# Recurrent block: both square roots together, the gate branch in five banks, its output gated in pairs of blocks

## The chip, the cores and the metric

The kernel runs on one core of one Trainium2 chip. The metric is device time in microseconds (us) of one execution; of several runs the median is taken.

## What is computed

Two layers of a decoder trunk on one sequence of 256 tokens with 1024 channels, all in float32. The first layer is attention and a dense feed-forward block; the second is a recurrent block and a feed-forward block of eight experts of which each token takes two. The change lies in the recurrent block alone. With D_RNN = 1280, in ten blocks of 128 channels, the reference has there:

```
proj = h @ w_in
gate_branch, u = proj[..., :D_RNN], proj[..., D_RNN:]
conv = conv_b + sum_j u_pad[:, j:j + s] * conv_w[j]            # width 4, causal
r = sigmoid(einsum(conv blocks, w_a) + b_a)
i = sigmoid(einsum(conv blocks, w_x) + b_x)
log_a = -RG_C * r * softplus(-lam)
a = exp(log_a)
mult = sqrt(-expm1(2 * log_a))
hs = linear recurrence over s of (a, mult * i * conv)
y = gelu(gate_branch) * hs
return y @ w_out
```

## The kernel before

Each matrix product is made of three float32r products: the operands are split into a rounded part (`whi`, `hThi`, `y` and so on, made by `ACTIVATE` on ScalarE at L386 or by `CAST` on VectorE at L388) and a remainder (`wlo`, made by a subtraction on VectorE at L389), and `mm3` (L403 to L405) adds up high times high, low times high and high times low. All weights come through one stream, `ws`: SyncE loads pages of two pieces of 128x1024 into six buffers, `step` splits the pieces ahead of their use into pairs of tiles, and `ws.done` gives a used pair back and splits the next. The program's text is the order: each engine runs its instructions in the order in which the code issues them and waits for semaphores of the others.

The loop at L841 has 20 rounds. Rounds 0 to 9 make the branch `u` (weights "lu"), its convolution and the gates r and i, two rounds late. Rounds 10 to 19, called m = 0 to 9 here, make the gate branch (weights "lg"): each product is 128x256, two of them share one PSUM bank, and `gbk[m]` keeps the bank until `gelu(m)` (L827) has read both halves into `ge`. The banks come from `wbank()`, a ring of four named "B" that the convolution and gate products use too.

Beside these matmuls the table `beside` puts, round by round, what the other engines do: `exp_tanh` (ScalarE) makes a and, in `rg`, what stands under the root; `recur(g)` for the two groups of five blocks takes the root on ScalarE (L808), multiplies twice on VectorE (L809, L810) and scans along the sequence (L812); `gelu` takes a bank; and `gated(a, z)` multiplies the scan's blocks a to z-1 by `ge` (L819, VectorE), rounds the product into the tile `y` (L386, ScalarE) and makes the remainder (L389, VectorE). Behind `beside`, `ws.done` splits the next weights, on ScalarE too unless m is 2, 4 or 6. ScalarE loads a table when the function changes to one of another set: roots and GeLU are in different sets, rounding is in every set.

After the loop comes `gated(8, 10)`, and then the output projection: ten weights "lo", called n = 0 to 9 here, of 12 matmuls each, three into each of four banks. Its banks (`y_banks`) are, in the order in which each weight writes them, `y0`, `y1` and two named `t`. `gate_rows` (L336) stands behind n = 4. The last two weights are kept for `finish`, which also keeps TensorE busy with a few repeated matmuls (`warm`, L424) while the norm is taken. Then the expert layer follows.

The pieces that set the order:

```
    ws.act = m not in (2, 4, 6)
    ws.done(ada=4)
...
    def y_banks():
        return [[bank("y0"), bank("y1")], [bank("t", 2), bank("t", 2)]]
```

Of the kernel before, what the change touches and what calls it, by code (L numbers as in the profile page):

```python
# [13 lines left out]
AF = mybir.ActivationFunctionType  # L14
# [116 lines left out]
def trunk_kernel(ctx, tc, xin, cbc, sm_d, at_d, wd, wm, out, stage=9):  # L131
    nc = tc.nc
    ctx.enter_context(tc.manual_schedule())
    V, A, T, G, SY = nc.vector, nc.scalar, nc.tensor, nc.gpsimd, nc.sync
# [7 lines left out]
    def bank(tag, bufs=1, dt=F32, shape=(P, 512)):  # L142
        return ps.tile(list(shape), dt, name=tag, tag=tag, bufs=bufs)

    def wbank():
        return bank("B", 4)
# [177 lines left out]
    def gate_cols(layer, which, gi):  # L324
        g = gcol["g"] = tmp.tile([P, 8], F32, name="gcol", bufs=1)
        m, bias = mods(layer, which)
        V.tensor_tensor(g, m, bias, op=ALU.add)
        V.tensor_tensor(g, g, norm_g(layer, gi), op=ALU.mult)
# [16 lines left out]
    def rstd(parts):  # L345
        v = tmp.tile([P, 1], F32, name="var", bufs=4)
        V.scalar_tensor_tensor(v, parts[:, 0:1], EPS, parts[:, 1:2], op0=ALU.add, op1=ALU.add)
        r = tmp.tile([P, 1], F32, name="rstd", bufs=4)
        G.tensor_tensor(r, v, mhalf[:, 0:1], op=ALU.pow)
        return r  # L350

    def sumsq(src_halves):
        parts = tmp.tile([P, 2], F32, name="parts", bufs=4)
        for h in range(2):
            sq = tmp.tile([P, 512], BF16, name="sq", bufs=1)
            A.activation(sq, src_halves[h], AF.Square, scale=1.0 / 32, accum_out=parts[:, h:h + 1])
        return parts
# [26 lines left out]
    def split(hi, lo, v32, act=False):  # L384
        if act:
            A.activation(hi, v32, AF.Copy)  # L386
        else:
            V.tensor_copy(hi, v32)  # L388
        V.tensor_tensor(lo, v32, hi.bitcast(F32), op=ALU.subtract)  # L389
# [17 lines left out]
    def wstat(o, w, hi, lo):  # L407
        wh, wl = w[:2]
        for k in range(KT):
            c = slice(k * P, (k + 1) * P)  # L410
            mm3(o, wh[:, c], wl[:, c], hi[:, k], lo[:, k], k == 0, k == KT - 1)
# [112 lines left out]
    s4 = const.tile([P, N_RNN], F32, name="s4")  # L524
# [45 lines left out]
    for i in range(16):  # L570
        w = ws.next()
        kind, j = w[2]
        b = wbank()
# [180 lines left out]
    def spare(tag, w=2 * SUB, pool=None, bufs=1):  # L754
# [6 lines left out]
    rg, aa = [[poolR.tile([P, 5, S], F32, name=f"{t}{g}", tag=f"{t}{g}") for g in range(2)]  # L761
              for t in ("rg", "aa")]
# [6 lines left out]
    def conv_step(n, b):  # L769
        u = b[:, :S]  # L770
        cv = conv[:, n]
        A.activation(cv, u, AF.Identity, scale=cw[:, 30 + n:31 + n], bias=cb_[:, n:n + 1])
        for j in (2, 1, 0):
            sft = 3 - j
            V.scalar_tensor_tensor(cv[:, sft:], u[:, :S - sft], cw[:, j * 10 + n:j * 10 + n + 1], cv[:, sft:],
                                   op0=ALU.mult, op1=ALU.add)
# [3 lines left out]
    def conv_split(n):  # L780
        ch = poolR.tile([P, S], F32R, name="ch", bufs=2)
        cl = poolR.tile([P, S], F32R, name="cl", bufs=2)
        split(ch, cl, conv[:, n], True)
        chl[n] = ch, cl

    def gates_mm(n):
        w = axw[n // 4]
        b = wbank()
        ch, cl = chl.pop(n)
        for g in range(2):  # L790
            c = slice((n % 4) * 256 + g * P, (n % 4) * 256 + g * P + P)
            mm3(b[:, g * S:(g + 1) * S], w[0][:, c], w[1][:, c], ch, cl, True, True)
        return b

    def gates_act(n, b):
        A.activation(rg[n // 5][:, n % 5], b[:, :S], AF.Sigmoid, bias=C("rb_a")[:, n:n + 1])
        ig = poolR.tile([P, S], F32, name="ig", bufs=2)
        A.activation(ig, b[:, S:], AF.Sigmoid, bias=C("rb_x")[:, n:n + 1])
        V.tensor_tensor(conv[:, n], conv[:, n], ig, op=ALU.mult)
        if n in (3, 7, 9):  # L800
            ws.done()

    ys = {}

    def recur(g):

        r, a_, c = rg[g], aa[g], conv[:, 5 * g:5 * g + 5]
        A.activation(r, r, AF.Sqrt)  # L808
        V.scalar_tensor_tensor(r, a_, 1.0, r, op0=ALU.add, op1=ALU.mult)  # L809
        V.tensor_tensor(r, r, c, op=ALU.mult)  # L810
        V.memset(a_[:, :, 0:1], 0.0)
        V.tensor_tensor_scan(*[t.rearrange("p n s -> p (n s)") for t in (c, a_, r)], 0.0,  # L812
                             op0=ALU.mult, op1=ALU.add)

    def gated(a, z):
        g = a // 5
        if a % 5 == 0:
            ys[g] = [poolR.tile([P, 5, S], F32R, name="y", tag=f"{t}{g}") for t in ("rg", "aa")]
        V.tensor_tensor(conv[:, a:z], conv[:, a:z], ge[:, a:z], op=ALU.mult)  # L819
        split(*[t[:, a - 5 * g:z - 5 * g] for t in ys[g]], conv[:, a:z], True)  # L820

    def exp_tanh(f, dst, scale, g):
        for i in range(5):
            n = 5 * g + i
            A.activation(dst[g][:, i], rg[g][:, i], f, scale=scale[:, n:n + 1])

    def gelu(n):  # L827
        A.activation(ge[:, n:n + 2], gbk.pop(n).rearrange("p (a b) -> p a b", a=2), AF.Gelu_apprx_tanh)  # L828
# [1 line left out]
    beside = {  # L830
        2: [lambda: exp_tanh(AF.Exp, aa, s8, 0)],
        3: [lambda: exp_tanh(AF.Exp, aa, s8, 1), lambda: gate_cols(1, 2, 1)],
        4: [lambda: exp_tanh(AF.Tanh, rg, s4, 0)],
        5: [lambda: exp_tanh(AF.Tanh, rg, s4, 1), lambda: recur(0)],
        6: [lambda: gelu(0), lambda: gelu(2), lambda: gated(0, 4)],
        7: [lambda: recur(1), lambda: gelu(4), lambda: gated(4, 5)],
        8: [lambda: gelu(6), lambda: gated(5, 8)],
        9: [lambda: gelu(8)],
    }
    gbk = {}  # L840
    for n in range(2 * N_RNN):  # L841
        ws.cap = 5 if n < N_RNN else DENSE_AHEAD
        if n in (2, 6, N_RNN):
            axw.append(ws.next("ax"))
        if n < N_RNN:
            w = ws.next("lu")
            b = wbank()
            wstat(b[:, :S], w, hi, lo)
        else:
            m = n - N_RNN  # L850
            w = ws.next("lg")
            if m % 2 == 0:
                b = gbk[m] = wbank()
            wstat(b[:, (m % 2) * S:(m % 2 + 1) * S], w, hi, lo)
        if 2 <= n < N_RNN + 2:
            gb = gates_mm(n - 2)
        if 1 <= n <= N_RNN:
            conv_split(n - 1)
        if n < N_RNN:
            conv_step(n, b)  # L860
        if 2 <= n < N_RNN + 2:
            gates_act(n - 2, gb)
        if n < N_RNN:
            ws.done()
        else:
            for f in beside.get(m, []):
                f()
            ws.act = m not in (2, 4, 6)
            ws.done(ada=4)
# [615 lines left out]
    with tc.If(flag > 0):  # L1485
# [14 lines left out]
        for tt in range(2):  # L1500
            r = rstd(sumsq([x[:, tt, :512], x[:, tt, 512:]]))
# [5 lines left out]
        with tc.For_i(0, N_EXP) as e:  # L1507
# [17 lines left out]
            m = Moe(Stream(pg, kd), False)  # L1525
# [154 lines left out]
```

## Time and profile before

| | |
|---|---|
| median of three runs | 1446.88 us |
| the three runs | 1446.87, 1446.88 and 1448.28 us |
| the profiled execution, its own time | 1448.85 us |
| its span in the trace | 1447.0 us |
| busy in the span: TensorE / VectorE / ScalarE | 1386.4 / 900.6 / 708.3 us |
| mean granted TensorE clock | 0.989 |
| the stretch of the change | from 431.7 us (table load for a) to 488.8 us (last projection matmul) |

The times in the trace run from the start of the span. A row of a timeline tells when an instruction began and, in brackets, how long its engine had been idle and which instruction ended that. Instructions of one engine overlap a little: the distance of two starts is the price of one in a row of many, the duration is what another engine has to wait.

### The profile page before, as it was taken

The page shows a single profiled execution, that of the slowest core. Times are in us where ns is not written, and L with a number is a line of the kernel's source. Part 1 is how long each engine was busy: PE and PEld are TensorE (multiplying, and loading weights), DVE is VectorE, ACT ScalarE, POOL GpSimd, SP SyncE. Part 2 cuts the span into 40 slices and gives each one's busy share as a digit, 9 for nine tenths or more (in the row PEclk, how much of TensorE's full clock was granted, in tenths as well). Part 3 has the DMA queues.
Part 4 walks back from the last instruction along what each step waited for, and adds up shares of the span by engine and source line. Part 5 has one row for each costly group of instructions (what it writes and reads, how often), then busy time and mean ns, then how long its engine had stood idle before and what let it go on. Part 6 is the DMA issues. An engine that isn't in the chain of part 4 may idle for free.

```text
span 1447.0 us, 21766 instructions
## 1 busy us (share of the span) xinstructions
PE 1386.4 (96%) x8325; PEld 1025.5 (71%) x8325; DVE 900.6 (62%) x1277; ACT 708.3 (49%) x1030; POOL 45.9 (3%) x62
## 2 busy tenths in 40 slices
PE   4998999999898899999999999999999999999997
PEld 3895589999797678887777767766566566665652
DVE  6887588875698889888666766754333343333321
ACT  3535455444586677976565656743232232321312
POOL 0105300000000000000000000000000000000000
PEclk9999999999999999999999999999999999999999
DMA  9876578886254988699999999999999999998991
GB/s 392 318 271 238 221 274 324 337 313 259 89 181 169 357 323 306 225 359 365 372 397 402 410 386 420 384 382 406 409 391 402 391 365 404 391 404 334 381 371 57
DMA packets 76991, 476.86 MB, mean 330 GB/s; under 512 B 8528, under 2 KB 8528, under 8 KB 28880
## 3 DMA queue, kind: packets, MB, share of 16 engines
q1 hardware_dynamic: 76880, 475.40, 84.1%
q8 instruction: 67, 1.10, 0.3%
q14 instruction: 44, 0.36, 0.1%
HBM read 474.32 MB, written 1.05 MB: 329 GB/s over the span
## 4 chain that ended last, share of the span: by engine, by line
PE 54%; DMA 2%; DVE 1%; issue 1%; ACT 0%; ACTq 0%
PE B L1061 18%; PE y L1061 7%; PE B L403 7%; PE B L405 6%; PE B L404 6%; PE y L405 2%; PE y L403 2%; PE y L404 2%; PE t L1150 2%; DMA raw<-in_wm_dram 2%; PE t L1334 1%; DVE wlo L389 1%; PE t L1039 0%; PE t L1040 0%; PE B L1444 0%
## 5 line engine op out<-in xcount | busy, mean ns | idle before, releaser
L389 DVE TENSOR_TENSOR wlo<-raw,whi 128x1024 fp32r<-128x1024 f32 x459 | 551.2, 1222 | 278.8 <-ACT whi L386 234.4
L386 ACT ACTIVATE whi<-raw 128x1024 fp32r<-128x1024 f32 x456 | 473.3, 1057 | 263.9 <-PE B L405 181.5
L1061 PE MATMUL B<-raw,xTc 128*64 128x256 f32 x1792 | 205.3, 382 | 0.0
L403 PE MATMUL B<-hThi,whi 128*128 128x256 f32 x640 | 181.8, 284 | 2.7 <-ACT ge L828 1.7
L404 PE MATMUL B<-hTlo,whi 128*128 128x256 f32 x640 | 181.2, 283 | 0.6
L403 PE MATMUL B<-whi,xTh 128*128 128x512 f32 x448 | 181.1, 404 | 0.0
L405 PE MATMUL B<-hThi,wlo 128*128 128x256 f32 x640 | 179.2, 280 | 0.0
L404 PE MATMUL B<-wlo,xTh 128*128 128x512 f32 x448 | 177.1, 395 | 0.3 <-DVE wlo L389 0.2
L1061 PEld LDWEIGHTS B<-raw,xTc 128*64 128x64 f32 x1792 | 124.3, 137 | 74.5 <-issue 16.8
L405 PE MATMUL B<-whi,xTl 128*128 128x512 f32 x448 | 176.6, 394 | 0.0
L403 PEld LDWEIGHTS B<-hThi,whi 128*128 128x128 f32 x640 | 120.9, 189 | 4.1 <-ACT ge L828 1.9
L404 PEld LDWEIGHTS B<-hTlo,whi 128*128 128x128 f32 x640 | 120.6, 188 | 3.6 <-DVE hTlo L389 2.7
L405 PEld LDWEIGHTS B<-hThi,wlo 128*128 128x128 f32 x640 | 120.5, 188 | 0.0
L212 DVE CUSTOM_DVE_ANT_0 raw<-raw,cond 128x1024 f32<-128x1024 f32 x96 | 114.4, 1223 | 0.0
L403 PEld LDWEIGHTS B<-whi,xTh 128*128 128x128 f32 x448 | 84.1, 188 | 30.6 <-issue 12.8
L1061 PE MATMUL y<-raw,hTc 128*64 128x512 f32 x448 | 101.9, 596 | 0.0
L405 PEld LDWEIGHTS B<-whi,xTl 128*128 128x128 f32 x448 | 84.1, 188 | 19.4
L404 PEld LDWEIGHTS B<-wlo,xTh 128*128 128x128 f32 x448 | 84.2, 188 | 19.2 <-DVE wlo L389 2.0
L1138 ACT ACTIVATE sg<-B 128x512 f32<-128x512 f32 x35 | 20.8, 595 | 99.1 <-PE B L1061 99.1
L1061 PEld LDWEIGHTS y<-raw,hTc 128*64 128x64 f32 x448 | 30.6, 137 | 54.4 <-issue 52.3
L403 PE MATMUL y<-whi,hTh 128*128 128x512 f32 x168 | 67.4, 401 | 0.0
L405 PE MATMUL y<-whi,hTl 128*128 128x512 f32 x168 | 66.5, 396 | 0.2 <-DVE hTl L1161 0.2
(322 smaller groups left out, 1646.9 us busy)
## 6 DMA issues: line engine op xcount, KB each, us to landing
raw<-in_wm_dram SPq DMA_DIRECT2D x261, 1024.0 KB, 8.8
raw<-in_wd_dram SPq DMA_DIRECT2D x114, 1024.0 KB, 6.5
raw<-in_wm_dram SPq DMA_DIRECT2D x150, 512.0 KB, 8.3
x<-in_x_dram SPq DMA_DIRECT2D x1, 1024.0 KB, 5.2
out_dram<-res SPq DMA_DIRECT2D x4, 256.0 KB, 2.8
sm<-in_sm_dram SPq DMA_DIRECT2D x1, 548.5 KB, 6.8
cond<-in_c_dram SPq DMA_DIRECT2D x1, 512.0 KB, 6.0
at<-in_at_dram SPq DMA_DIRECT2D x1, 320.0 KB, 7.0
```

The source lines that it names most:

```text
L212: V.tensor_tensor_reduce(src, src, cond, 1.0, 0.0, op0=ALU.mult, op1=ALU.add, accum_out=modc[:, col:col + 1])
L386: A.activation(hi, v32, AF.Copy)
L389: V.tensor_tensor(lo, v32, hi.bitcast(F32), op=ALU.subtract)
L403: T.matmul(o, lh, rh, start=start, stop=False)
L404: T.matmul(o, lh, rl, start=False, stop=False)
L405: T.matmul(o, ll, rh, start=False, stop=stop)
L1061: T.matmul(o[64 * t:64 * t + 64], xs, w[:, t * n:t * n + n], start=start, stop=stop)
L1138: A.activation(g[t], ub[t], AF.Copy)
L1150: T.transpose(b[:, j * P:(j + 1) * P], a[t][:, j * P:(j + 1) * P], ident)
L1334: T.matmul(b, u.pt[t][r, tt * P:(tt + 1) * P], yr[r, j], start=j == 0, stop=j == 1)
```

## The change

The root becomes a function of its own, and both roots stand together in m = 5, the two calls that make what stands under them in m = 4. GeLU and gating are spread: one bank of GeLU and then the blocks that it completes, in six pieces of one or two blocks instead of four pieces of one to four. The second recurrence stands behind the first two pairs. The banks of m = 6 and m = 8 are `y0` and `y1` instead of two of the ring.

```
--- before.py
+++ after.py
@@ -802,10 +802,12 @@
 
     ys = {}
 
+    def root(g):
+        A.activation(rg[g], rg[g], AF.Sqrt)
+
     def recur(g):
 
         r, a_, c = rg[g], aa[g], conv[:, 5 * g:5 * g + 5]
-        A.activation(r, r, AF.Sqrt)
         V.scalar_tensor_tensor(r, a_, 1.0, r, op0=ALU.add, op1=ALU.mult)
         V.tensor_tensor(r, r, c, op=ALU.mult)
         V.memset(a_[:, :, 0:1], 0.0)
@@ -830,12 +832,12 @@
     beside = {
         2: [lambda: exp_tanh(AF.Exp, aa, s8, 0)],
         3: [lambda: exp_tanh(AF.Exp, aa, s8, 1), lambda: gate_cols(1, 2, 1)],
-        4: [lambda: exp_tanh(AF.Tanh, rg, s4, 0)],
-        5: [lambda: exp_tanh(AF.Tanh, rg, s4, 1), lambda: recur(0)],
-        6: [lambda: gelu(0), lambda: gelu(2), lambda: gated(0, 4)],
-        7: [lambda: recur(1), lambda: gelu(4), lambda: gated(4, 5)],
-        8: [lambda: gelu(6), lambda: gated(5, 8)],
-        9: [lambda: gelu(8)],
+        4: [lambda: exp_tanh(AF.Tanh, rg, s4, 0), lambda: exp_tanh(AF.Tanh, rg, s4, 1)],
+        5: [lambda: root(0), lambda: root(1), lambda: recur(0)],
+        6: [lambda: gelu(0), lambda: gated(0, 2)],
+        7: [lambda: gelu(2), lambda: gated(2, 4), lambda: recur(1)],
+        8: [lambda: gelu(4), lambda: gated(4, 5), lambda: gelu(6), lambda: gated(5, 7)],
+        9: [lambda: gelu(8), lambda: gated(7, 8)],
     }
     gbk = {}
     for n in range(2 * N_RNN):
@@ -850,7 +852,7 @@
             m = n - N_RNN
             w = ws.next("lg")
             if m % 2 == 0:
-                b = gbk[m] = wbank()
+                b = gbk[m] = wbank() if m < 6 else bank(("y0", "y1")[m // 2 - 3])
             wstat(b[:, (m % 2) * S:(m % 2 + 1) * S], w, hi, lo)
         if 2 <= n < N_RNN + 2:
             gb = gates_mm(n - 2)
```

ScalarE, from the split of the second output weight to the GeLU of m = 6 (before) and of m = 8 (the change). `whi` is a weight's rounded part, `y` the rounded gated product, `ge` the GeLU's output, `B`, `y0` and `y1` are PSUM banks. Before:

```order
L386 ACTIVATE whi_4428<-raw_4227 128x1024 [waits DMAHW7_49,DVE_49,PE_49]
L828 ACT_TABLE_LOAD
L828 ACTIVATE ge_3714<-B_4183 128x512
L828 ACTIVATE ge_3714<-B_4282 128x512 [waits PE_49]
L386 ACTIVATE y_4459<-conv_3665 128x1024 [waits DVE_49]
L808 ACT_TABLE_LOAD
L808 ACTIVATE rg1_3667<-rg1_3667 128x1280 [waits Activation_49]
L828 ACT_TABLE_LOAD
L828 ACTIVATE ge_3714<-B_4354 128x512 [waits PE_49]
L386 ACTIVATE y_4459<-conv_3665 128x256 [waits DVE_49]
L386 ACTIVATE whi_4503<-raw_4272 128x1024 [waits DMAHW0_49]
L828 ACTIVATE ge_3714<-B_4432 128x512 [waits PE_49]
```

The change, from the load of the GeLU table:

```order
L830 ACT_TABLE_LOAD
L830 ACTIVATE ge_3714<-B_4183 128x512
L386 ACTIVATE y_4459<-conv_3665 128x512 [waits DVE_49]
L830 ACTIVATE ge_3714<-B_4282 128x512 [waits PE_49]
L386 ACTIVATE y_4459<-conv_3665 128x512 [waits DVE_49]
L386 ACTIVATE whi_4502<-raw_4272 128x1024 [waits DMAHW0_49,PE_49]
L830 ACTIVATE ge_3714<-B_4354 128x512 [waits PE_49]
L386 ACTIVATE y_4459<-conv_3665 128x256 [waits DVE_49]
L830 ACTIVATE ge_3714<-y0_4433 128x512 [waits PE_49]
L386 ACTIVATE y_4536<-conv_3665 128x512 [waits DVE_49]
L386 ACTIVATE whi_4541<-raw_4272 128x1024
L830 ACTIVATE ge_3714<-y1_4506 128x512 [waits PE_49]
```

The second root and its table load are gone from between; the GeLU of m = 6 reads `y0` and stands behind the rounding of block 4, the GeLU of m = 8 reads `y1` and stands behind the rounding of blocks 5 and 6 and the split of the fifth output weight.

VectorE, from the first gate product on (before) and from the remainder of the third output weight on (the change). L809 to L812 (L811 to L814 in the change) are the second recurrence, whose scan prints as a SCALAR_TENSOR_TENSOR of 128x1280. Before:

```order
L819 TENSOR_TENSOR conv_3665<-conv_3665,ge_3714 128x1024 [waits DVE_49,Activation_49]
L389 TENSOR_TENSOR y_4460<-conv_3665,y_4459 128x1024 [waits Activation_49]
L388 CAST whi_4464<-raw_4227 128x1024 [waits PE_49]
L389 TENSOR_TENSOR wlo_4465<-raw_4227,whi_4464 128x1024 [waits DVE_49,PE_49]
L809 SCALAR_TENSOR_TENSOR rg1_3667<-aa1_3669,rg1_3667 128x1280 [waits Activation_49]
L810 TENSOR_TENSOR rg1_3667<-rg1_3667,conv_3665 128x1280 [waits DVE_49]
L811 MEMSET aa1_3669 128x5
L812 SCALAR_TENSOR_TENSOR conv_3665<-aa1_3669,rg1_3667 128x1280 [waits DVE_49]
L819 TENSOR_TENSOR conv_3665<-conv_3665,ge_3714 128x256 [waits Activation_49]
L389 TENSOR_TENSOR y_4460<-conv_3665,y_4459 128x256 [waits Activation_49]
L389 TENSOR_TENSOR wlo_4504<-raw_4272,whi_4503 128x1024 [waits DMAHW0_49,PE_49,Activation_49]
L819 TENSOR_TENSOR conv_3665<-conv_3665,ge_3714 128x768 [waits Activation_49]
```

The change:

```order
L389 TENSOR_TENSOR wlo_4465<-raw_4227,whi_4464 128x1024 [waits DVE_49,PE_49]
L821 TENSOR_TENSOR conv_3665<-conv_3665,ge_3714 128x512 [waits Activation_49]
L389 TENSOR_TENSOR y_4460<-conv_3665,y_4459 128x512 [waits Activation_49]
L811 SCALAR_TENSOR_TENSOR rg1_3667<-aa1_3669,rg1_3667 128x1280
L812 TENSOR_TENSOR rg1_3667<-rg1_3667,conv_3665 128x1280 [waits DVE_49]
L813 MEMSET aa1_3669 128x5
L814 SCALAR_TENSOR_TENSOR conv_3665<-aa1_3669,rg1_3667 128x1280 [waits DVE_49]
L389 TENSOR_TENSOR wlo_4503<-raw_4272,whi_4502 128x1024 [waits DMAHW0_49,PE_49,Activation_49]
L821 TENSOR_TENSOR conv_3665<-conv_3665,ge_3714 128x256 [waits Activation_49]
L389 TENSOR_TENSOR y_4460<-conv_3665,y_4459 128x256 [waits Activation_49]
L821 TENSOR_TENSOR conv_3665<-conv_3665,ge_3714 128x512 [waits Activation_49]
L389 TENSOR_TENSOR y_4537<-conv_3665,y_4536 128x512 [waits Activation_49]
```

The second recurrence has the gating of blocks 2 and 3 ahead of it, and behind it the remainder of the fourth output weight now stands ahead of the product of block 4.

TensorE, at the end of the gate branch and the start of the output projection; `y0_...` and `y1_...` with an output weight (`whi_4384` or `whi_4389`) are its first two banks, and `y_4459` and `y_4460` are the two parts of its other operand. Before:

```order
L404 MATMUL B_4507<-hTlo_3671,whi_4350 128x256
L405 MATMUL B_4507<-hThi_3670,wlo_4351 128x256
L403 MATMUL y0_4580<-whi_4384,y_4459 128x512 [waits Activation_49]
L404 MATMUL y0_4580<-wlo_4385,y_4459 128x512 [waits DVE_49]
L405 MATMUL y0_4580<-whi_4384,y_4460 128x512 [waits DVE_49]
L403 MATMUL y1_4581<-whi_4384,y_4459 128x512
L404 MATMUL y1_4581<-wlo_4385,y_4459 128x512
```

The change:

```order
L404 MATMUL y1_4506<-hTlo_3671,whi_4350 128x256
L405 MATMUL y1_4506<-hThi_3670,wlo_4351 128x256
L403 MATMUL y0_4586<-whi_4389,y_4459 128x512 [waits DVE_49,Activation_49]
L404 MATMUL y0_4586<-wlo_4390,y_4459 128x512 [waits DVE_49]
L405 MATMUL y0_4586<-whi_4389,y_4460 128x512 [waits DVE_49]
L403 MATMUL y1_4587<-whi_4389,y_4459 128x512 [waits Activation_49]
L404 MATMUL y1_4587<-wlo_4390,y_4459 128x512
```

The last matmuls of the gate branch write `y1` instead of a bank of the ring, and the first matmuls into `y0` and into `y1` have waits that they did not have.

## Rows read from the trace of the kernel before

**Rows 1.** The page, busy time by engine: us, share of the span, instructions.

```profile
PE 1386.4 (96%) x8325; PEld 1025.5 (71%) x8325; DVE 900.6 (62%) x1277; ACT 708.3 (49%) x1030; POOL 45.9 (3%) x62
```

**Rows 2.** Windows from 453 to 489 us and from 525 to 1425 us. Columns: the stretch and its length, then busy us and instructions of PE, PEld, DVE, ACT and POOL, the granted TensorE clock (1.00 is 2.4 GHz, 0.50 is 1.2 GHz), the DMA share and GB/s.

```profile
453.00:489.00 36.00, 32.98 (x142) 25.88 (x141) 31.22 (x39) 20.73 (x28) 0.55 (x1) 0.95 0.59 224
525.00:1425.00 900.00, 897.90 (x5169) 609.87 (x5169) 494.70 (x532) 422.34 (x522) 0.00 (x0) 1.00 0.94 372
```

**Rows 3.** What the matmuls of TensorE waited for between 420 and 520 us: line and output tile, what released it, us in total, times, longest.

```profile
PE B L403 <- ACT ge L828: 1.7, 1, 1.7
...
PE y L403 <- ACT whi L386: 1.2, 1, 1.2
PE y L404 <- DVE wlo L389: 0.8, 1, 0.8
...
PE y L405 <- DVE y L389: 0.5, 1, 0.5
```

**Rows 4.** Timeline of ScalarE (ACT) from the first root on. Columns: start in us, duration in us, engine, line, operation, output and input with their shapes; in brackets the idle time before it and what ended that.

```profile
442.09 1.28 ACT L808 ACT_TABLE_LOAD   x1
443.38 1.27 ACT L808 ACTIVATE rg<-rg 128x1280 f32<-128x1280 f32 x1
444.56 1.04 ACT L386 ACTIVATE whi<-raw 128x1024 fp32r<-128x1024 f32 x1
445.62 1.28 ACT L828 ACT_TABLE_LOAD   x1
446.92 1.09 ACT L828 ACTIVATE ge<-B 128x512 f32<-128x512 f32 x2
...
463.28 0.42 ACT L386 ACTIVATE y<-conv 128x256 fp32r<-128x256 f32 x1 [4.85 <-DVE conv L819]
...
464.55 0.58 ACT L828 ACTIVATE ge<-B 128x512 f32<-128x512 f32 x1
...
473.91 0.63 ACT L386 ACTIVATE y<-conv 128x512 fp32r<-128x512 f32 x1 [3.89 <-DVE conv L819]
```

**Rows 5.** Timeline of VectorE (DVE) over the same stretch, same columns.

```profile
444.69 1.49 DVE L809 SCALAR_TENSOR_TENSOR rg<-aa,rg 128x1280 f32<-128x1280 f32 x1 [1.14 <-ACT rg L808]
...
447.76 2.82 DVE L812 TENSOR_TENSOR_SCAN conv<-aa,rg 128x1280 f32<-128x1280 f32 x1
450.50 1.20 DVE L389 TENSOR_TENSOR wlo<-raw,whi 128x1024 fp32r<-128x1024 f32 x1
...
455.10 0.69 DVE L388 CAST whi<-raw 128x1024 fp32r<-128x1024 f32 x1
455.89 1.23 DVE L389 TENSOR_TENSOR wlo<-raw,whi 128x1024 fp32r<-128x1024 f32 x1
457.04 1.49 DVE L809 SCALAR_TENSOR_TENSOR rg<-aa,rg 128x1280 f32<-128x1280 f32 x1
...
462.84 0.40 DVE L819 TENSOR_TENSOR conv<-conv,ge 128x256 f32<-128x256 f32 x1
...
469.76 1.22 DVE L212 CUSTOM_DVE_ANT_0 raw<-raw,cond 128x1024 f32<-128x1024 f32 x1
...
473.19 0.68 DVE L819 TENSOR_TENSOR conv<-conv,ge 128x512 f32<-128x512 f32 x1
474.57 0.69 DVE L389 TENSOR_TENSOR y<-conv,y 128x512 fp32r<-128x512 f32 x1 [0.70 <-ACT y L386]
```

**Rows 6.** Timeline of TensorE's matmuls (PE) over the same stretch, same columns. The starts tell the pace; the ends are modelled.

```profile
445.61 0.28 PE L405 MATMUL B<-hThi,wlo 128*128 128x256 f32 x1
447.57 0.39 PE L403 MATMUL B<-hThi,whi 128*128 128x256 f32 x1 [1.68 <-ACT ge L828]
...
453.21 0.28 PE L405 MATMUL B<-hThi,wlo 128*128 128x256 f32 x1
453.98 0.50 PE L403 MATMUL y<-whi,y 128*128 128x512 f32 x1 [0.49 <-ACT y L386]
...
457.69 0.39 PE L403 MATMUL y<-whi,y 128*128 128x512 f32 x1
...
460.49 0.39 PE L403 MATMUL y<-whi,y 128*128 128x512 f32 x1
...
465.95 0.50 PE L404 MATMUL y<-wlo,y 128*128 128x512 f32 x1 [0.76 <-DVE wlo L389]
...
467.00 0.63 PE L405 MATMUL y<-whi,y 128*128 128x512 f32 x1
...
469.99 0.58 PE L403 MATMUL y<-whi,y 128*128 128x512 f32 x1
...
472.97 1.95 PE L336 MATMUL B<-sm,gcol 128*128 128x128 f32 x16
474.68 0.48 PE L403 MATMUL y<-whi,y 128*128 128x512 f32 x1
...
488.77 3.36 PE L424 MATMUL B<-whi 128*128 128x512 f32 x14
```

**Rows 7.** Two windows of 2 us each, from 112 and from 468 (columns as in group 2).

```profile
112.00:114.00 2.00, 0.00 (x0) 0.00 (x0) 0.94 (x6) 1.38 (x7) 0.22 (x1) 0.50 0.67 209
468.00:470.00 2.00, 2.00 (x7) 1.51 (x6) 2.00 (x3) 2.00 (x3) 0.00 (x0) 0.50 0.00 0
```

**Rows 8.** Timeline of TensorE around 115 us, in the attention layer.

```profile
115.02 0.80 PE L638 MATMUL B<-dg,pr 128*128 128x128 f32 x2 [4.18 <-DVE mx L614]
```

More of the change, by code (lines that the diff above doesn't have):

```diff
@@ L803, in trunk_kernel, with root @@
     ys = {}
+    def root(g):
+        A.activation(rg[g], rg[g], AF.Sqrt)
     def recur(g):
         r, a_, c = rg[g], aa[g], conv[:, 5 * g:5 * g + 5]
-        A.activation(r, r, AF.Sqrt)
         V.scalar_tensor_tensor(r, a_, 1.0, r, op0=ALU.add, op1=ALU.mult)
@@ L832, in trunk_kernel @@
         3: [lambda: exp_tanh(AF.Exp, aa, s8, 1), lambda: gate_cols(1, 2, 1)],
[L833 to L838, printed above, removed]
+        4: [lambda: exp_tanh(AF.Tanh, rg, s4, 0), lambda: exp_tanh(AF.Tanh, rg, s4, 1)],
+        5: [lambda: root(0), lambda: root(1), lambda: recur(0)],
+        6: [lambda: gelu(0), lambda: gated(0, 2)],
+        7: [lambda: gelu(2), lambda: gated(2, 4), lambda: recur(1)],
+        8: [lambda: gelu(4), lambda: gated(4, 5), lambda: gelu(6), lambda: gated(5, 7)],
+        9: [lambda: gelu(8), lambda: gated(7, 8)],
     }
@@ L852, in trunk_kernel @@
             if m % 2 == 0:
-                b = gbk[m] = wbank()
+                b = gbk[m] = wbank() if m < 6 else bank(("y0", "y1")[m // 2 - 3])
             wstat(b[:, (m % 2) * S:(m % 2 + 1) * S], w, hi, lo)
```

## The prediction

> **What bounds the kernel now.** I read the page's busy lines first, then the windows of the second half, then the list of what TensorE waited for around the change, and last the three engines' timelines through that stretch. TensorE (PE) is busy 96% of the span [rows 1]. In the 900 us from 525 to 1425, nearly all of the expert layer, it is busy 897.90 us [rows 2]: there is next to no room to swallow a delay that arrives from ahead. So time won or lost by TensorE in the recurrent block should reach the end almost whole. Between 453 and 489, where the output projection runs, it is busy 32.98 of 36 us at a mean granted clock of 0.95 [rows 2], so there is something to win. The reader is to see four waits [rows 3]: 1.7 us for a GeLU that had to free a PSUM bank, 0.5 for a VectorE product, 1.2 and 0.8 for a weight split that came late. The rest of the loss is clock: after those late splits the output matmuls stand 7 intervals in 2.99 us (467.00 to 469.99), 0.427 us each, against 12 in 2.80 us (457.69 to 460.49), 0.233 each [rows 6]. The granted clock there is 0.50, the 1.2 GHz level [rows 7].
>
> **The roots and the table loads (ScalarE).** Everything up to the first root stands as before, so it starts at 443.38 again. The next instruction starts 1.18 later [rows 4]; now it is the second root, and the weight split that stood there moves from 444.56 to 445.74. The load of the GeLU table follows 1.06 after it, at 446.80, and GeLU(0) 1.30 later, at 448.10 [rows 4]. That is 1.18 us later than 446.92; nobody waits for it any more, because the last bank of the gate branch is no longer GeLU(0)'s. The second switch to the root and back goes: two loads of 1.28 [rows 4]. I cost this at nothing, because they lay in ScalarE's wait for VectorE: its next piece of output, at 463.28, had waited 4.85 us for VectorE's product [rows 4].
>
> **The bank wait that goes.** The matmuls on either side of it start 1.96 us apart (445.61 and 447.57), two on end 0.12, so 1.84 is won [rows 6]. The gate branch's last matmul moves from 453.21 to 451.37.
>
> **The chain through VectorE.** The first recurrence needs the first root only: it starts at 444.69 and its scan ends at 450.58, the weight split behind it starts at 450.50 as now [rows 5]. Then a gate product of 512 columns at 451.62 (0.68), its rounding on ScalarE (0.63), the remainder on VectorE (0.69) [rows 4, 5]: to about 453.65. The cast and split at 455.10 to 457.04 take 1.94 [rows 5]: to 455.56. The second pair, again 0.68, 0.63 and 0.69 in turn: 457.55. So the second recurrence starts half a us later than now (457.04). It takes what the first took, 5.89 us (444.69 to 450.58) [rows 5]: 463.4. The split of the fourth output weight now stands ahead of the product of block 4: 1.12, to 464.5, then that product, 0.40, and its rounding, 0.42: 465.3 [rows 4, 5]. Only behind these stands **GeLU(6)**, 0.58 [rows 4]: it ends at about 465.8. The product of blocks 5 and 6 (0.68), its rounding (0.63), a weight split (1.0) and only then **GeLU(8)**: 468.6.
>
> **The wait that is added.** The fourth and fifth banks of the gate branch are y0 and y1, the first two of the output projection. In the order of TensorE the first matmul into y0 now waits for ScalarE as well as VectorE, and the first into y1 has a wait for ScalarE that it did not have. The only ScalarE work that these can need and that was not needed before is the reading of the two banks: GeLU(6) and GeLU(8). TensorE has nothing else to do, because everything behind is the same projection. So it stops at 451.5, runs three matmuls at 465.85, stops again, and goes on at 468.65. Before, the projection had begun at 453.98 [rows 6].
>
> From 468.65 at full clock: nine matmuls left of the first weight (9 times 0.233 is 2.10), four weights of 2.80 (11.2), the gate rows (472.97 to 474.68, 1.71), the other five weights (474.68 to 488.77, 14.09) [rows 6]: 497.75. The weight splits are early enough here: the remainder of the fourth, for which TensorE waited until 465.95 before [rows 6], is finished at 464.5 and wanted at 476, the fifth at 469.4 and at 479. Against 488.77 this is **9.0 us later**, with the 1.84 already credited and all four waits of [rows 3] gone.
>
> **The clock.** After 4.18 us without a matmul TensorE resumed at the low level (the row at 115.02; the window before it shows 0.50) [rows 7, 8]; a 14 us hole will do the same. A low stretch like that of 467.00 to 470.4 is 3.4 us of work at 0.427 instead of 0.233 and costs 1.55 [rows 6]. The first three matmuls of it, 1.28 us, lie in front of a wait and cost nothing, so I take the remaining 2.1 us, that is 1.0. No low stretch behind the wait would be 0, a second whole one 2.55.
>
> The sum is 9.0 + 1.0 = **10.0 us**. The profiled execution took 1448.85 us (span 1447.0), which is 1.97 above the median of the runs, 1446.88; I set the difference on the median: **1456.9 us**. Bounds: no low stretch, and all the 2.1 us that TensorE idles later (900 less 897.90) given back, leaves 6.9; with 0.8 for durations that I read too long, 6.1. Upward, 9.0 and 2.55, and 1.5 for one late split behind the hole, give 13.1. That is 1453.0 to 1460.0.
>
> **The rivals.**
> (1) The banks do not hold TensorE: it starts the projection when the first pair is ready, by 454, which decides it. Then the next limits are splits behind the scan: the fourth weight's remainder at 464.5 instead of 465.95 [rows 6], the fifth's at 469.4 (GeLU(8)'s neighbour), and the sixth's at 474.65: from 469.4 two modulation products of 1.15 (from 469.76 on) [rows 5], a gate product with its rounding, 0.9, and a split of 1.0 and 1.22. The sixth starts at 474.68 now [rows 6]: no change, 1446.9. Even the 1.84 is then lost to VectorE. Against it: the added wait in TensorE's order. For it: only that the listing names the engine and not the instruction. The Trainium skill's page "PSUM — Partial Sum Buffer" (section "PSUM bank collisions raise a hardware error"), has the rule to guard a PSUM bank as a whole with a semaphore while two engines use it, which speaks for a wait here; the trace agrees, with 1.7 us that TensorE waited for a GeLU to leave a bank [rows 3].
> (2) Faster: ScalarE's loads were on the path. Two of 1.28 less [rows 4] give 2.56, 1444.3. Against it: the 4.85 us wait beside them. The Trainium skill, "ScalarE: Activation LUTs" (section "Table sets: the hidden batching unit"), has the rule to do all calls of one table set together, which is this change. Its section "What ACT_TABLE_LOAD costs" gives about 2.66 us for a switch, with a drain; by that it would be 5.3 us and 1441.6. The trace differs: from the load's start to the root's start is 1.29 [rows 4], with no drain to be seen.
> (3) The hole costs more than the sum: the clock stays low for two stretches or longer. 9.0 + 2.55 gives 1458.4, a third 1460.0.
>
> **How the numbers follow.** Forecast, the banks hold TensorE and one low stretch at most: 0.80. Rival 3: 0.12. Rival 1: 0.05. Rival 2: 0.03. A measurement of this kernel can tell about 0.2%, 2.9 us, from no change. The forecast and rival 3 are both slower by more, 0.92; rival 1 is the same, 0.05; rival 2 with what it wins beside is faster, 0.03. The range leaves out rivals 1 and 2 and the far end of 3.
>
> **What would show it.** In the changed kernel's waits of TensorE a line for the y banks on ScalarE's GeLU, 14.4 us and 1.5 us, and none for the gate branch's bank; ScalarE with two loads less; GeLU(6) ending near 465.8 and GeLU(8) near 468.6; the granted clock at 0.50 around 468; the warming matmuls of L424 at 498 to 500 instead of 488.77; and the same distance to the end of the span from there on. It is wrong if the first projection matmul starts before 455, if the wait is there but the weights behind it arrive late, or if the span grows by much less than those matmuls move.

## The result, and the profile after

The change takes 1458.14 us (median of 6 runs, 1457.58 to 1459.29), the kernel before 1447.30 (median of 6, 1446.68 to 1448.75): 10.84 us more, ratio 1.0077, interval 1.0067 to 1.0087. The forecast was 1456.9 in 1453 to 1460. The profiled execution of the change took 1457.84 us, its span is 1456.0 us.

The kernel got slower although TensorE was busy half a microsecond less than before [rows 1], with the same number of matmuls. The page's busy line, after:

```profile
PE 1385.9 (95%) x8325; PEld 1025.7 (70%) x8325; DVE 900.9 (62%) x1281; ACT 705.6 (48%) x1030; POOL 45.9 (3%) x62
```

So the question is where it stood. This is what its matmuls of the projection (L403 to L405, `y`) waited for between 420 and 530 us (tile and line, releaser, us in total, times, longest); the four waits of [rows 3] are gone, and one line has come:

```profile
PE y L403 <- ACT ge L830: 15.5, 2, 14.3
```

The reader sees two waits of a projection matmul for a GeLU, 14.3 and 1.2 us. The next views show which ones.

**How the two traces are laid over each other.** The first root starts at 441.64 here and at 443.38 in the trace of before [rows 4], although ScalarE and VectorE run the same instructions ahead of it. Over the ten profiled executions of this study, of all kernels, that start lies between 441.3 and 444.2. Below, times are therefore counted from the start of the first root. "The way" is the distance from there to the first warming matmul of L424 behind the projection: 45.39 us before (443.38 to 488.77, [rows 4, 6]).

ScalarE, from the first root on (start, duration, engine, line, operation, output and input; in brackets its idle time and what ended that):

```profile
441.64 2.44 ACT L806 ACTIVATE rg<-rg 128x1280 f32<-128x1280 f32 x2
443.98 1.04 ACT L386 ACTIVATE whi<-raw 128x1024 fp32r<-128x1024 f32 x1
445.04 1.28 ACT L830 ACT_TABLE_LOAD   x1
446.34 0.60 ACT L830 ACTIVATE ge<-B 128x512 f32<-128x512 f32 x1
...
463.15 0.42 ACT L386 ACTIVATE y<-conv 128x256 fp32r<-128x256 f32 x1 [6.58 <-DVE conv L821]
463.47 0.58 ACT L830 ACTIVATE ge<-y 128x512 f32<-128x512 f32 x1
464.81 0.63 ACT L386 ACTIVATE y<-conv 128x512 fp32r<-128x512 f32 x1 [0.76 <-DVE conv L821]
465.35 1.04 ACT L386 ACTIVATE whi<-raw 128x1024 fp32r<-128x1024 f32 x1
466.29 0.58 ACT L830 ACTIVATE ge<-y 128x512 f32<-128x512 f32 x1
```

The two roots, one split, one table load and GeLU(0) follow each other without a gap; the load and the first GeLU are 1.30 apart. Far behind stand the two GeLUs of the borrowed banks, now reading `y`: GeLU(6) from 463.47, GeLU(8) from 466.29. In front of GeLU(6) stands the rounding of block 4, which waited 6.58 us for VectorE's product. VectorE, same columns, shows why:

```profile
442.94 1.49 DVE L811 SCALAR_TENSOR_TENSOR rg<-aa,rg 128x1280 f32<-128x1280 f32 x1 [1.14 <-ACT rg L806]
...
455.78 1.48 DVE L811 SCALAR_TENSOR_TENSOR rg<-aa,rg 128x1280 f32<-128x1280 f32 x1
...
462.70 0.42 DVE L821 TENSOR_TENSOR conv<-conv,ge 128x256 f32<-128x256 f32 x1
```

The second recurrence starts 12.84 us after the first (before: 12.35, [rows 5]), and the product of block 4 comes behind its scan and the remainder of the fourth weight. TensorE, same columns:

```profile
449.52 0.28 PE L405 MATMUL y<-hThi,wlo 128*128 128x256 f32 x1
464.10 0.80 PE L403 MATMUL y<-whi,y 128*128 128x512 f32 x1 [14.30 <-ACT ge L830]
...
465.12 0.63 PE L405 MATMUL y<-whi,y 128*128 128x512 f32 x1
466.92 0.80 PE L403 MATMUL y<-whi,y 128*128 128x512 f32 x1 [1.17 <-ACT ge L830]
...
470.93 0.60 PE L403 MATMUL y<-whi,y 128*128 128x512 f32 x1
```

The last matmul of the gate branch starts at 449.52. Then nothing runs until GeLU(6) has ended; three matmuls fill `y0`, and at 466.92 the first into `y1` starts, 0.05 after GeLU(8) has ended. The warming matmuls come at 498.11:

```profile
498.11 2.24 PE L424 MATMUL B<-whi 128*128 128x512 f32 x9
```

The way is 56.47 us, 11.08 more than before. The clock in windows of 2 us (columns as in [rows 2]; the granted clock is the third value from the end):

```profile
462.00:464.00 2.00, 0.00 (x0) 0.00 (x0) 1.52 (x3) 0.85 (x2) 0.00 (x0) 0.50 0.00 0
468.00:470.00 2.00, 2.00 (x6) 1.61 (x5) 2.00 (x5) 0.00 (x0) 0.00 (x0) 0.50 0.60 160
470.00:472.00 2.00, 2.00 (x7) 1.56 (x6) 0.99 (x3) 1.36 (x2) 0.00 (x0) 0.66 1.01 414
472.00:474.00 2.00, 2.00 (x10) 1.59 (x10) 1.53 (x2) 0.44 (x1) 0.00 (x0) 1.00 1.02 426
```

It is 0.50, the 1.2 GHz level, in the hole and for the matmuls behind it, and back at 1.00 from about 471.3. The nine matmuls that are left of the first weight (466.92 to 470.93, 0.446 apart) and the first of the next run at the low level, not the five of 0.427 that fill the prediction's 2.1 us. Next to nothing is given back later. From L424 to the end of the span it was 958.23 us (1447.0 less 488.77) and is 957.89 (1456.0 less 498.11), and in the same 900 us of the expert layer TensorE was busy 897.90 us [rows 2] and is now

```profile
535.00:1435.00 900.00, 898.77 (x5178) 611.17 (x5179) 494.04 (x532) 421.65 (x522) 0.00 (x0) 1.00 0.95 372
```

### The profile page after: what moved, and what is told of

Its sections match the earlier page's. It is cut to its first block, busy times and chain, and to the rows that moved or that the text cites. A ratio compares the mean times of both kernels' runs of the same rounds, so it can differ in the third digit from the quotient of the medians.

```text
span 1456.0 us, 21770 instructions
## 1 busy us (share of the span) xinstructions
PE 1385.9 (95%) x8325; PEld 1025.7 (70%) x8325; DVE 900.9 (62%) x1281; ACT 705.6 (48%) x1030; POOL 45.9 (3%) x62
## 4 chain that ended last, share of the span: by engine, by line
PE 55%; DVE 1%; DMA 1%; issue 0%; ACT 0%; ACTq 0%
PE B L1063 19%; PE y L1063 7%; PE B L403 7%; PE B L405 6%; PE B L404 6%; PE y L403 2%; PE y L405 2%; PE y L404 2%; PE t L1152 2%; PE t L1336 1%; DVE wlo L389 1%; DMA raw<-in_wm_dram 1%; PE t L1041 0%; PE t L1042 0%; PE B L1446 0%
## 5 line engine op out<-in xcount | busy, mean ns | idle before, releaser
L403 PE MATMUL B<-whi,xTh 128*128 128x512 f32 x448 | 181.3, 405 | 0.0
L405 PE MATMUL B<-whi,xTl 128*128 128x512 f32 x448 | 176.8, 395 | 0.0
L403 PE MATMUL B<-hThi,whi 128*128 128x256 f32 x608 | 172.7, 284 | 0.5 <-ACT v L397 0.5
L404 PE MATMUL B<-hTlo,whi 128*128 128x256 f32 x608 | 172.2, 283 | 0.7
L405 PE MATMUL B<-hThi,wlo 128*128 128x256 f32 x608 | 170.2, 280 | 0.0
L404 PEld LDWEIGHTS B<-hTlo,whi 128*128 128x128 f32 x608 | 114.3, 188 | 3.8 <-DVE hTlo L389 3.1
L403 PEld LDWEIGHTS B<-hThi,whi 128*128 128x128 f32 x608 | 114.7, 189 | 1.7 <-ACT v L397 1.0
L405 PEld LDWEIGHTS B<-hThi,wlo 128*128 128x128 f32 x608 | 114.4, 188 | 0.0
L403 PEld LDWEIGHTS B<-whi,xTh 128*128 128x128 f32 x448 | 84.1, 188 | 30.4 <-issue 12.8
L405 PEld LDWEIGHTS B<-whi,xTl 128*128 128x128 f32 x448 | 84.2, 188 | 19.4
L403 PE MATMUL y<-whi,hTh 128*128 128x512 f32 x168 | 67.5, 402 | 0.0
L405 PE MATMUL y<-whi,hTl 128*128 128x512 f32 x168 | 66.5, 396 | 0.0
```

The lines of the kernel that those rows point to most:

```text
L403: T.matmul(o, lh, rh, start=start, stop=False)
L404: T.matmul(o, lh, rl, start=False, stop=False)
L405: T.matmul(o, ll, rh, start=False, stop=stop)
```

## The experiments

**Theory A**, the forecast's: the whole loss comes from lending `y0` and `y1` to the gate branch, because GeLU(6) and GeLU(8) stand on ScalarE behind what waits for the second scan; about 9 us of hole and the rest clock. Roots together and gating in pairs are worth nothing. **Rival B:** the new order on VectorE and ScalarE costs the time itself, and the banks only show it. **Rival C:** the table loads are on the path, so that roots together win 2.6 us, hidden by the loss of the banks. The first four kernels take the change apart.

**e1_ring: the change without the lent banks.**

```diff
-                b = gbk[m] = wbank() if m < 6 else bank(("y0", "y1")[m // 2 - 3])
+                b = gbk[m] = wbank()
```

> The change with one part undone: the GeLU banks of m = 6 and m = 8 come from the ring of four again; roots together and gating in pairs stay. Measure: us from the start of the first root to the first warming matmul of L424; 45.39 before (443.38 to 488.77), 56.47 in the change (441.64 to 498.11). Theory A (the lent banks are the loss): the 14.3 and 1.2 us holes go; the gate branch waits about 3.0 us for GeLU(0), which stands 1.2 us later than before, and VectorE's splits bound the projection, so 45 to 47 us, no more than 1.5 us from before in total time. Rival B (the order of roots and pairs on ScalarE and VectorE is the loss): 51 to 56 us and 5 to 11 us slower than before. Rival C (roots and pairs win, and the banks hid it): 42 to 44 us, 2 to 3 us faster than before.

Measured: 1448.32 us against 1447.37, ratio 1.0002 (0.9993 to 1.0011). Both holes are gone, the way is 46.54 us. What TensorE waited for in that stretch:

```profile
PE y L404 <- DVE wlo L389: 3.3, 5, 1.3
PE B L403 <- ACT ge L830: 2.8, 1, 2.8
PE y L403 <- ACT whi L386: 0.8, 1, 0.8
```

The new order of VectorE and ScalarE alone costs nothing that the time shows, so rival B falls. The waits of before are back, and two are longer: the bank of GeLU(0) costs 2.8 instead of 1.7 us [rows 3], since the second root now stands ahead of that GeLU, and VectorE's remainders cost 3.3 instead of 0.8.

**e2_banks: the kernel before, with the lent banks alone.**

```diff
-                b = gbk[m] = wbank()
+                b = gbk[m] = wbank() if m < 6 else bank(("y0", "y1")[m // 2 - 3])
```

> The kernel before with one part of the change alone: the GeLU banks of m = 6 and m = 8 are y0 and y1; roots and gating as before. Theory A: GeLU(6) and GeLU(8) end where they do in the trace of before, some 21.7 and 25.7 us after the first root's start (465.13 and 469.08 less 443.38), the projection goes on behind them, and with one or two low clock stretches the way from first root to L424 is 55.5 to 58 us: 10 to 12.5 us slower than before, as the whole change or a little worse. Rival B: 45 to 47 us, no slower than before.

Measured: 1460.31 against 1447.37, ratio 1.0085 (1.0071 to 1.0098); the way is 57.25 us. By the medians that is 12.94 us more, 0.4 over the upper end of what was expected; the way is within it. The two waits of the change are there, 13.6 and 2.3 us:

```profile
PE y L403 <- ACT ge L828: 15.9, 2, 13.6
```

One edit makes the loss, and taking it out of the change (e1_ring) removes the loss: A holds from both sides.

**e3_roots: the kernel before, with the roots together alone.**

```diff
+    def root(g):
+        A.activation(rg[g], rg[g], AF.Sqrt)
...
-        A.activation(r, r, AF.Sqrt)
...
-        4: [lambda: exp_tanh(AF.Tanh, rg, s4, 0)],
-        5: [lambda: exp_tanh(AF.Tanh, rg, s4, 1), lambda: recur(0)],
+        4: [lambda: exp_tanh(AF.Tanh, rg, s4, 0), lambda: exp_tanh(AF.Tanh, rg, s4, 1)],
+        5: [lambda: root(0), lambda: root(1), lambda: recur(0)],
```

> The kernel before with the two roots together (and the two calls that make what stands under them in m = 4); banks and gating as before. Two table loads of 1.28 us are gone from ScalarE. Theory A: they lay in waits for VectorE, GeLU(0) comes 1.2 us later and the gate branch's bank with it, VectorE's chain stays: 45 to 46 us from first root to L424, within 0.7 us of before. Rival C (the loads were on the path): 42.8 us, 2.6 us faster; by the price with a drain 5.3 faster. Rival B: 47 us or more.

Measured: 1447.46 against 1447.37, ratio 1.0002 (0.9993 to 1.0011); the way is 45.12 us. ScalarE:

```profile
441.43 1.28 ACT L806 ACT_TABLE_LOAD   x1
442.72 2.44 ACT L806 ACTIVATE rg<-rg 128x1280 f32<-128x1280 f32 x2
...
446.12 1.28 ACT L830 ACT_TABLE_LOAD   x1
447.42 1.08 ACT L830 ACTIVATE ge<-B 128x512 f32<-128x512 f32 x2
452.21 1.06 ACT L386 ACTIVATE y<-conv 128x1024 fp32r<-128x1024 f32 x1 [3.71 <-DVE conv L821]
...
462.61 0.42 ACT L386 ACTIVATE y<-conv 128x256 fp32r<-128x256 f32 x1 [8.85 <-DVE conv L821]
```

Two loads are left where there were four. The two that are gone, and the second root, stood between these two pieces of output, and the second piece now waits 8.85 us for VectorE's product instead of 4.85 [rows 4]: what ScalarE saves, it waits. Rival C falls. The Trainium skill, "ScalarE: Activation LUTs" (section "Table sets: the hidden batching unit"), asks to do all calls of one set together; followed here to the letter, it changed the time by nothing that can be measured. Its section "What ACT_TABLE_LOAD costs" gives 2.66 us for a switch with its drain; the trace disagrees, with 1.30 us from the load's start (446.12) to that of the GeLU behind it (447.42).

This run shows a second thing. Its granted clock stayed up through the whole stretch:

```profile
443.00:489.00 46.00, 40.29 (x209) 32.72 (x209) 40.11 (x47) 23.26 (x34) 0.55 (x1) 1.00 0.56 220
```

Before, the clock was low around 468 [rows 7], and 1.5 us of work were lost to it by the prediction's own rate. Yet the way without that is only 0.27 us shorter. TensorE:

```profile
465.28 0.50 PE L404 MATMUL y<-wlo,y 128*128 128x512 f32 x1 [0.76 <-DVE wlo L389]
...
469.24 0.50 PE L404 MATMUL y<-wlo,y 128*128 128x512 f32 x1 [0.76 <-DVE wlo L389]
```

It comes to the remainder of the fourth weight 22.56 us after the root (before: 465.95 less 443.38, 22.57, [rows 6]), although it waited 2.8 us for GeLU(0)'s bank instead of 1.7 [rows 3]: that loss is made up for by then. From here on it runs at the full clock, and at the next weight it waits again, 0.76 us, for a remainder that VectorE has yet to make. Before there was one such wait [rows 3], here there are two. So of the 1.5 us, 0.76 went into waiting for VectorE at once.

**e4_ahead: the change, with GeLU(6) and GeLU(8) ahead of the gating of blocks 4 to 7.**

```diff
-        8: [lambda: gelu(4), lambda: gated(4, 5), lambda: gelu(6), lambda: gated(5, 7)],
-        9: [lambda: gelu(8), lambda: gated(7, 8)],
+        8: [lambda: gelu(4), lambda: gelu(6)],
+        9: [lambda: gelu(8), lambda: gated(4, 5), lambda: gated(5, 7), lambda: gated(7, 8)],
```

> The change with the gating of block 4 and of blocks 5 to 7 moved behind GeLU(8), so that GeLU(6) and GeLU(8) stand on ScalarE ahead of everything that waits for the second scan; banks, roots and pairs as in the change. Theory A (what costs is that the two GeLUs stand behind the second scan): GeLU(8) ends about 16 us after the first root's start instead of 25.2, TensorE's hole is 7 to 8 us instead of 14.3 and the second one under 1 us, and the way from first root to L424 is 46 to 49 us: 1 to 3.5 us slower than before. If the lent banks cost by themselves, wherever the GeLUs stand: 54 us or more, 9 us slower than before.

Measured: 1449.70 against 1447.37, ratio 1.0018 (1.0009 to 1.0027); the way is 47.61 us. GeLU(6) and GeLU(8) no longer wait for the scan (ScalarE):

```profile
456.51 0.59 ACT L830 ACTIVATE ge<-y 128x512 f32<-128x512 f32 x1
...
457.94 0.59 ACT L830 ACTIVATE ge<-y 128x512 f32<-128x512 f32 x1
466.62 0.42 ACT L386 ACTIVATE y<-conv 128x256 fp32r<-128x256 f32 x1 [8.09 <-DVE conv L821]
```

The two GeLUs of 456.51 and 457.94 are those of m = 6 and m = 8. GeLU(8) ends at 458.53, 16.85 us after the root instead of 25.23, and the wait of 8.09 us stands behind it instead of in front. TensorE's first projection matmul:

```profile
457.15 0.79 PE L403 MATMUL y<-whi,y 128*128 128x512 f32 x1 [7.32 <-ACT ge L830]
```

The same banks are lent, and half the hole and about four fifths of the loss are gone (2.33 us are left of 10.84; less than the hole, because the waits of [rows 3] are gone here too). So it is not the lending by itself, but the place that the bank's last reader has in ScalarE's order.

**e5_warm: the change, with 55 repeated matmuls in the hole.** They write into a bank of the ring that nobody reads, to keep TensorE busy between the gate branch and the projection.

```diff
     gated(8, 10)
+    warm(wbank(), ws.ready[0][0], 55)
     Y = y_banks()
```

> The change with 55 matmuls of 128x512 added on TensorE between the gate branch and the output projection, into a free bank that nobody reads: 12.8 us of work at full clock inside the 14.3 us hole. Nothing else moves, the first projection matmul still waits for GeLU(6). Measure as before: 56.47 us from first root to L424 in the change, 45.39 before. Theory A with its clock term: the granted clock stays at the 2.4 GHz level, the projection's first weight takes 2.1 us for nine matmuls instead of 4.0, so 54.2 to 54.6 us, about 2 us faster than the change and 9 slower than before. If the low clock costs nothing that the hole would not cost anyway: 56.5, as the change; if the waits themselves depend on TensorE's idling: anything under 53.

Measured: 1458.54 against 1446.98, ratio 1.0086 (1.0072 to 1.0100); the way is 56.04 us. This missed: 0.43 us of way came back of the 2 that were expected, and nothing that the time shows. The repeated matmuls ended 1.8 us too early, so two gaps remained, and the clock fell all the same, only later:

```profile
PE y L403 <- ACT ge L830: 3.7, 2, 1.9
```

In the windows of 2 us from 464 on (columns as in [rows 2]):

```profile
464.00:466.00 2.00, 0.96 (x3) 0.48 (x3) 1.25 (x3) 1.24 (x3) 0.00 (x0) 1.00 0.00 0
466.00:468.00 2.00, 0.82 (x3) 0.68 (x4) 1.75 (x3) 1.12 (x2) 0.00 (x0) 0.91 0.00 0
468.00:470.00 2.00, 2.00 (x7) 1.52 (x6) 2.00 (x3) 0.00 (x0) 0.00 (x0) 0.50 0.39 82
```

TensorE ran three matmuls in each of the first two windows, on either side of the second gap, and from 468 on the clock is at 0.50. So with the long hole filled, the clock fell behind two short gaps.

**e7_warm72: the same with 72 repeated matmuls.** They reach beyond the end of GeLU(6).

> As the run with 55 added matmuls, but with 72: 16.8 us of work, from the end of the gate branch to 24.8 us after the first root's start, just short of the end of GeLU(8) at 25.2. With 55 TensorE had two gaps of 1.8 us around the first three projection matmuls and the granted clock fell at 25.9 us all the same (466.92 to 467.81 in that trace), so the way was 56.04 us, not 54.2 to 54.6. Theory A with its clock term: with the gaps filled the clock stays at the 2.4 GHz level and the projection runs 12 matmuls per weight at 0.233: 24.8 + 2.8 + 11.2 + 1.7 + 14.1 = 54.6 us from first root to L424, 1.9 less than the change and 9.2 more than before. If the low clock is no loss of its own: 56 us or more.

Measured: 1456.38 against 1447.67, ratio 1.0060 (1.0047 to 1.0074); the way is 54.51 us. The listing of waits has no GeLU any more, and the clock stays up:

```profile
466.00:468.00 2.00, 1.91 (x9) 1.25 (x8) 1.85 (x2) 0.60 (x2) 0.00 (x0) 1.00 0.04 8
468.00:470.00 2.00, 2.00 (x10) 1.61 (x9) 2.00 (x5) 0.00 (x0) 0.00 (x0) 1.00 0.73 205
```

The first matmul into `y1` still starts 25.3 us after the root (466.65 less 441.34), as in the change (466.92 less 441.64). So the hole without the clock costs 54.51 less 45.39, that is 9.1 us, and the clock in the change's profile 56.47 less 54.51, that is 2.0.

**after_again: the change once more, on the chip of e7_warm72.**

> The change once more, on the same chip as the run with 72 added matmuls, so that the two can be set side by side: 56.5 us from first root to L424, give or take 0.5, two holes of 14.3 and 1.2 us, 10 to 12 us slower than before in total.

Measured: 1459.97 against 1447.67, ratio 1.0084 (1.0070 to 1.0097). The way is 57.30 us and the medians are 12.30 us apart, each 0.3 over the upper end of what was expected. The two waits are those of the change, 14.30 and 1.17 us; the difference is the clock, still low here at 474 and beyond, 30 us after the root (444.18):

```profile
472.00:474.00 2.00, 2.00 (x6) 1.52 (x6) 1.23 (x4) 1.16 (x2) 0.00 (x0) 0.50 0.97 401
474.00:476.00 2.00, 2.00 (x7) 1.57 (x6) 1.76 (x2) 0.20 (x1) 0.00 (x0) 0.58 1.00 377
```

So the clock's price is 57.30 less 54.51 here, 2.8 us. The medians of these two kernels, taken side by side, are 3.59 us apart (1459.97 less 1456.38), somewhat more than either profile gives.

**e6_order: the lesson turned round.** Several edits to the change stand together here. The last two banks of the gate branch are the projection's two `t`, which each weight writes last instead of first; GeLU(0) to GeLU(6) stand ahead of the second recurrence; and the blocks are gated four, one and three at a time. In m = 6 the weight split goes to ScalarE as well.

```diff
-        6: [lambda: gelu(0), lambda: gated(0, 2)],
-        7: [lambda: gelu(2), lambda: gated(2, 4), lambda: recur(1)],
-        8: [lambda: gelu(4), lambda: gated(4, 5), lambda: gelu(6), lambda: gated(5, 7)],
-        9: [lambda: gelu(8), lambda: gated(7, 8)],
+        6: [lambda: gelu(0), lambda: gelu(2), lambda: gelu(4), lambda: gated(0, 4)],
+        7: [lambda: gelu(6), lambda: recur(1)],
+        9: [lambda: gelu(8), lambda: gated(4, 5), lambda: gated(5, 8)],
...
-                b = gbk[m] = wbank() if m < 6 else bank(("y0", "y1")[m // 2 - 3])
+                b = gbk[m] = wbank() if m < 6 else bank("t", 2)
...
-            ws.act = m not in (2, 4, 6)
+            ws.act = m not in (2, 4)
```

> A version meant to beat both: roots together as in the change; all GeLUs on ScalarE ahead of what waits for the second scan (GeLU(0), GeLU(2), GeLU(4) and blocks 0 to 3 gated in one piece in m = 6, GeLU(6) and the second recurrence in m = 7, GeLU(8) ahead of the gating of blocks 4 to 7 in m = 9); the fourth and fifth banks of the gate branch are the two t banks, which each weight of the projection writes last; the cast of m = 6 goes to ScalarE. Theory A: no wait for a bank longer than 1.2 us, the 1.84 us of the gate branch's bank wait won, then VectorE's chain of splits and gating bounds the projection as before: 43.5 to 45 us from first root to L424, 0.5 to 2 us faster than before. If lending the projection's banks costs wherever the GeLUs stand: 47 us or more. If VectorE's chain were no bound, the projection would end 5 us earlier than before: 40 us.

Measured: 1445.30 (11 runs) against 1446.98 (15 runs), ratio 0.9989 (0.9980 to 0.9998); the way is 43.71 us, 1.68 shorter than before. It is ahead of both kernels, by an interval that lies just below 1. No matmul waits for a bank; the waits there are for the gated product's two parts and for a remainder:

```profile
PE y L403 <- ACT y L386: 2.4, 1, 2.4
...
PE y L405 <- DVE y L389: 0.5, 1, 0.5
...
PE y L404 <- DVE wlo L389: 0.4, 1, 0.4
```

That the choice of `t` matters is seen on ScalarE, where the last GeLU of the gate branch reads its bank:

```profile
455.67 0.58 ACT L830 ACTIVATE ge<-t 128x512 f32<-128x512 f32 x1
```

It ends at 456.25, when the projection has been running since 452.49; TensorE writes the second `t` only from 456.67, and had this bank been `y1`, wanted at 454.11, it would have waited for it. What each of the other edits gives by itself was not run.

What is left is one wait for the first gated product, 2.4 us, and behind it the low clock for some 3 us, in windows of 2 us (columns as in [rows 2]):

```profile
454.00:456.00 2.00, 2.00 (x6) 1.55 (x6) 2.00 (x2) 2.00 (x3) 0.00 (x0) 0.51 0.20 29
456.00:458.00 2.00, 2.00 (x8) 1.50 (x7) 1.93 (x4) 0.25 (x1) 0.00 (x0) 0.63 0.82 311
458.00:460.00 2.00, 2.00 (x10) 1.64 (x9) 2.00 (x1) 0.00 (x0) 0.00 (x0) 1.00 0.46 184
```

## Why the prediction was right

The mechanism was right, and so was the size of its main term; the clock's term was too small. The forecast lies 1.2 us under the measured time: 0.8 of that is the sum (10.0 against 10.84), and 0.4 the kernel before, whose median was 1446.88 then and 1447.30 here. The steps follow one by one. Where a time of the change is compared with a predicted one, the 1.74 us are added by which its first root starts earlier.

- **What bounds the kernel: TensorE, and nothing swallows a delay behind the block.** Right: 11.08 us more way became 10.84 us more time.
- **The banks hold TensorE until GeLU(6) and GeLU(8), both behind the second scan.** Right, and shown from both sides by e1_ring and e2_banks. The chain was 465.8 and 468.6; measured were 465.79 and 468.61. The waits were to be 14.4 and 1.5 us and are 14.30 and 1.17. The Trainium skill, "PSUM — Partial Sum Buffer" (section "PSUM bank collisions raise a hardware error"), has the rule to guard PSUM with semaphores, in its simple version by the whole bank; the trace agrees in that TensorE stood 14.30 us for a bank whose reader had not come, but it cannot tell a guard by bank from one by address, because the matmul writes all that the GeLU reads.
- **The hole costs 9.0 us.** Right: 9.1 in e7_warm72.
- **The clock costs 1.0 us.** The mechanism was right, the size was not: 2.0 us in one profile (56.47 less 54.51), 2.8 in the other (57.30 less 54.51). The step took one stretch of 3.4 us that begins with the matmul at the first wait's end. Low are in fact the 7.3 us from 464.10 to 471.35 here, and 9.0 us in after_again (466.64 to 475.60); the second wait lies inside and does not end it. The upper bound of the term, 2.55, held the first and not the second. The range, which left room for a second stretch and for a late split, held both.
- **The loads at nothing, because ScalarE waits for VectorE there.** Right, shown by e3_roots.
- **The 1.84 us at the gate branch's bank.** Won in the change, which has no such wait. But it is won by the two borrowed banks and not by the order: with the ring kept, the wait is 2.8 us (e1_ring).
- **The splits early enough behind the hole.** Right: no wait for a weight stands in the change's list.
- **Rival 1** said that without a hold VectorE would be the bound and the time the same. e1_ring is that case: 46.54 us of way and 1.0002. Set beside e3_roots it gives the part of the pairs, 46.54 less 45.12, about 1.4 us of way, which the time of the two kernels does not resolve. The terms of its last sum add up to 474.82, not 474.65, which changes nothing in it.
- **Rival 2** is refuted by e3_roots. **Rival 3**, the clock low for two stretches or longer, is what happened on that point: 7.3 and 9.0 us are two stretches of 3.4 and more, where the forecast had one at most. The time of 1458.14 is nearer to rival 3's 1458.4 than to the forecast's 1456.9, and its price for the clock, 2.55, lies between the 2.0 and the 2.8 measured. It had a chance of 0.12 against 0.80; both share the mechanism and most of the range, so the time alone would not have told them apart.
- **The first reading of before** was half right. "The rest of the loss is clock" holds for the rows, but the time was not to be had there: e3_roots ran that stretch at the full clock and gained 0.27 us.

What stays open: why the low stretch lasts 7.3 us in one execution and 9.0 in another, which of e6_order's edits wins its 1.68 us, and how much it would gain if its wait of 2.4 us went.

## What to carry to other kernels

Before lending a PSUM bank from one stage to the next, write down the last instruction that reads it and what stands in front of that in its engine's order; lend the banks that the next stage writes last, and move their readers ahead of anything that waits (14.3 us of hole became 7.3 by moving two readers, and no matmul waited for a bank in e6_order, where other banks were lent as well). An edit that shortens an engine which then waits for another one wins little until the other is shorter: here the two table loads won nothing and the full clock 0.27 us. Price a hole as its length and the low clock behind it, taken from a run at either level.

## What the runs showed that was not expected

- The clock's price varies between executions of one program: low for 7.3 us and for 9.0 us behind the same two waits, 0.8 us of way.
- The clock fell to 0.50 behind two gaps of 1.8 us around three matmuls, although the 12.7 us ahead were filled (e5_warm), and in e6_order behind a wait of 2.4 us and one of 0.5. In e1_ring and e3_roots, whose longest wait was 2.8 us, the granted clock was 1.00 through the stretch.
- With the same instructions ahead, the start of the first root varied by 2.8 us between executions (441.34 to 444.18), and by 2.5 between two of the same kernel (441.64 and 444.18).
